# Seven products for eight in the down projection of an encoder step's feed-forward part, with new block closings and buffers

## The chip, the cores and the metric

The kernel runs on one core of one Trainium2 chip. Its time is the device time of one execution in microseconds. The engines that matter here are TensorE (PE, the matrix products; PEld in the profile is its loading of stationary operands), VectorE (DVE), ScalarE (ACT), GpSimd (POOL) and the queue of SyncE (SP), which issues nearly all transfers. Work on an engine runs in the order in which it was placed in that engine's queue.

## The reference, cut to what matters

One layer of a streaming encoder is computed for 2048 prompt tokens and 32 sample tokens, 2080 in all, with a model width of 1024 and a feed-forward width of 2816. Each of its three sub-layers has a norm before and a norm after, and is added to the residual:

```python
xp = xp + rmsnorm(mix_output(oa, ob, r, g_gla_out[l], w_o[l]), g_post_mix[l])
...
xp = xp + rmsnorm(mem_attention(rmsnorm(xp, g_pre_mem[l]), mk, mv, w_mq[l], w_mo[l]), g_post_mem[l])
...
def swiglu(h, w_gate, w_up, w_down):
    return (jax.nn.silu(h @ w_gate) * (h @ w_up)) @ w_down
xp = xp + rmsnorm(swiglu(rmsnorm(xp, g_pre_ffn[l]), w_ffn_gate[l], w_ffn_up[l], w_ffn_down[l]), g_post_ffn[l])
```

The change lies in the last of these, the feed-forward part, and in the few lines before it that end the memory attention. Everything is in 32-bit floats.

## The kernel before, in words

Every large product is made of three: each operand is split into a rounded part (type fp32r) and the remainder, and `mm3` (L130 to L137) issues high by high, high by low and low by high. `split` (L77 to L82) makes the two parts: ACT casts (L78), and DVE or POOL subtracts (L82). Where no engine is named, `lo_set` and `flip` let POOL and DVE take turns.

The feed-forward part starts at L1018. Tokens are in three blocks (`CF`), and each block is two halves of 348 or 346 tokens, called `ci` 0 and 1. Activations are feature-major: features on the 128 partitions, tokens along the row. The feed-forward width is 22 tiles of 128 features, taken as 11 groups `g` of two tiles.

For a group, `gate_up` makes the gate product and the up product. Each of them is one `unit` (L1117): a 2 by 2 block product by the seven-product scheme (Strassen's in Winograd's form), over two row halves and two column halves of the weights, and two feature halves and two token halves of the activations. The seven combinations of the activations are made once per block (`ffn_ops`, tiles `mf`, from the loaded `hr`). The seven combinations of the weights are made for each unit (`unit_w`: the raw tiles `wg_r` and `wu_r` are changed in place by four sums on DVE, lines L1039 and L1042, and split seven times into `wg_s` and `wu_s`, 512 columns each). Each of the seven products is 12 matmuls into PSUM banks X, Y and Z; the first three values are copied out by ACT (L1122 to L1126, tile `pg_c` or `pu_c`), the next ones are summed by DVE. After the up unit, DVE multiplies the four quarters (L1150, `sg`), and each is split into `u`, with POOL making the remainder.

`down` (L1177) adds a group to the block's accumulator `acc` in the plain way: for each token half and each of the 8 output tiles, 6 matmuls (two feature tiles by three products) into one bank, and a DVE sum into `acc` straight from PSUM (L1042; a copy, L1185, for the first group). That is 96 matmuls for a group, 288 for a group with its two units, so 264 with the seven-product units: 84 for gate, 84 for up, 96 for down. The loop emits the down product of group g-1 after the units of group g.

At the end of blocks 0 and 1, `finish` closes the block for each token half: squares on ACT, their sum on DVE (`ssq`), a matmul with ones, the root, the scaling (DVE, L1222), the residual (`x2r`, added by POOL), a transposition to token-major rows by PE (`yt`, L1230, with the copies out of PSUM at L1231), and the store. In the last block the second half closes the same way and the first one by `finish_rows`, which transposes before it scales.

The order within each queue is set when the program is built: a planner runs the emitted instructions by priority through a timeline of its own and places each when its operands would be ready. `high_priority` raises a block of code; weights have it. So down products are used as filler between the matmuls of the units.

SBUF is laid out by pools in the order in which they are opened. The feed-forward pools lie over those of the memory attention, so a tile's place decides which earlier work it has to wait for.

Of the kernel before, what the change touches and what calls it, by code (L numbers as in the profile page):

```python
# [45 lines left out]
def encoder_step(ctx, tc, ins, outs):  # L46
# [806 lines left out]
    with ExitStack() as ph:  # L853
# [149 lines left out]
        out = []  # L1003
        for b in range(len(CB)):
            mo, heads = mem_attn(b)
            fill = [partial(mem_q, b + 1, mv, m) for m in range(KT)] if b + 1 < len(CB) else out
# [4 lines left out]
            out = mem_out(b, mo)  # L1011
            if b != len(CB) - 2:
                for it in out:
                    it()
# [5 lines left out]
    UB, WRB, WSB, SGB = 3, 4, 8, 5  # L1020
    with ExitStack() as ph:
        def pool(name, bufs):
            return ph.enter_context(tc.tile_pool(name=name, bufs=bufs, **RW))
# [10 lines left out]
        pd = ph.enter_context(tc.tile_pool(name="cpd", bufs=6, space=PSUM, **RW))  # L1034
# [9 lines left out]
        def stage(name):  # L1044
            return gp.tile([P, HK, 348], F32, tag="stage", name=name)

        def ffn_raw(b):

            s, n = CF[b]
            raw = {}  # L1050
            for kh, c in ((0, 0), (0, 1), (1, 1), (1, 0)):
# [6 lines left out]
        def ffn_ops(b, raw):  # L1058

            n = CF[b][1]  # L1060
            b11, b12, b22, b21 = raw[0, 0], raw[0, 1], raw[1, 1], raw[1, 0]
            ops = []

            def put(src, eng):
                m_ = mps[len(ops)].tile([P, 2, HK, 348], F32R, tag="mov", name=f"mf{b}_{len(ops)}")
                split(m_[:, 0, :, :n], m_[:, 1, :, :n], src, eng)
                ops.append((m_[:, 0, :, :n], m_[:, 1, :, :n]))

# [10 lines left out]
            put(b21, DVE)  # L1079
            return ops  # L1080

        def unit_w(src, g, name):

            with tc.high_priority(offset=PRI):
                raw = []
                for kh in range(2):
                    r = wp.tile([P, HK, 2, P], F32, tag="wraw", name=f"{name}_r{kh}", bufs=WRB)
                    SP.dma_start(r, src[kh * 512 : kh * 512 + 512, g * 256 : g * 256 + 256].rearrange("(k p) m -> p k m", p=P).rearrange("p k (a m) -> p k a m", a=2))
                    raw.append(r)
                a11, a21, a12, a22 = raw[0][:, :, 0], raw[0][:, :, 1], raw[1][:, :, 0], raw[1][:, :, 1]  # L1090
                ops = []

                def put(v, eng=None):
                    w = wp.tile([P, 2, HK, P], F32R, tag="wsp", name=f"{name}_s{len(ops)}", bufs=WSB)
                    split(w[:, 0], w[:, 1], v, eng)
# [15 lines left out]
        def prod(ps, w, m, first, last):  # L1111
            mm3(ps, [((w[0][:, k], w[1][:, k]), (m[0][:, k], m[1][:, k])) for k in range(HK)], first, last, not first)

        def small(pool, tag, name, bufs):
            return pool.tile([P, 348], F32, tag=tag, name=name, bufs=bufs)

        def unit(w, m, n, name, dst):  # L1117

            X, Y, Z = (pd.tile([P, 512], F32, tag="dense", name=f"{name}_{c}")[:, :n] for c in "XYZ")
            cp = [small(sp, "cp", f"{name}_c{i}", 4)[:, :n] for i in range(3)]  # L1120
            prod(X, w[0], m[0], True, True)
            ACT.copy(cp[0], X)  # L1122
            prod(Y, w[1], m[1], True, True)
            ACT.copy(cp[1], Y)
            prod(X, w[2], m[2], False, True)
            ACT.copy(cp[2], X)  # L1126
            prod(Y, w[3], m[3], False, True)
            add(DVE, dst[0, 1], cp[2], Y)
            prod(X, w[4], m[4], False, True)
            add(DVE, dst[1, 1], cp[1], X)  # L1130
            prod(Z, w[5], m[5], True, True)
            add(DVE, dst[0, 0], cp[0], Z)
            prod(X, w[6], m[6], False, True)
            return X

        QS = ((0, 1), (1, 1), (0, 0), (1, 0))
        ops = ffn_ops(0, ffn_raw(0))
        for b, (s, n) in enumerate(CF):
            ssqs, silu = {}, []
            acc = [xp.tile([P, KT, 348], F32, tag="acc", name=f"acc{b}_{ci}") for ci in range(2)]  # L1140
            def gate_up(g, own=False):
                sg = {q: small(sp, "sg", f"sg{b}_{g}_{q[0]}{q[1]}", SGB)[:, :n] for q in QS}
                up = {q: small(up_, "up", f"up{b}_{g}_{q[0]}{q[1]}", 3)[:, :n] for q in QS[:3]}
                X = unit(unit_w(ins["w_ffn_gate"][0], g, f"wg{b}_{g}"), ops, n, f"pg{b}_{g}", sg)
                for q in QS:
                    silu.append(ACT.activation(sg[q], sg[q] if q != (1, 0) else X, AF.Silu))
                up[1, 0] = unit(unit_w(ins["w_ffn_up"][0], g, f"wu{b}_{g}"), ops, n, f"pu{b}_{g}", up)
                u = [(gp if own else uu).tile([P, 2, 2, 348], F32R, tag="stage" if own else "u", name=f"u{b}_{g}_{j}") for j in range(2)]
                for q in QS:
                    DVE.tensor_tensor(out=sg[q], in0=sg[q], in1=up[q], op=ALU.mult)  # L1150
                    ut = u[q[0]][:, :, q[1], :n]
                    split(ut[:, 0], ut[:, 1], sg[q], POOL)
                return u

            def down_w(f):

                row = []
                with tc.high_priority(offset=PRI):
                    raw_d = wp.tile([P, KT, P], F32, tag="wraw", name=f"wd{b}_{f}_r", bufs=WRB)
                    SP.dma_start(raw_d, ins["w_ffn_down"][0][f * P : (f + 1) * P, :].rearrange("p (k m) -> p k m", k=KT))  # L1160
                    for q in range(2):
                        w = wp.tile([P, 2, HK, P], F32R, tag="wsp", name=f"wd{b}_{f}_{q}", bufs=WSB)
# [4 lines left out]
            def square(ci, m):  # L1167

                if m == 0:
                    ssqs[ci] = small(np_, "nacc", f"ssq{b}_{ci}", 2)[:, :n]  # L1170
                    ACT.activation(ssqs[ci], acc[ci][:, m, :n], AF.Square)
                else:
                    sq = small(np_, "nsq", f"sq{b}_{ci}_{m}", 1)[:, :n]
                    ACT.activation(sq, acc[ci][:, m, :n], AF.Square)
                    add(DVE, ssqs[ci], ssqs[ci], sq)

            def down(gs, us, cis=(1, 0), dn=None):  # L1177
                dn = dn or [down_w(2 * g + j) for g in gs for j in range(2)]
                us = [ut for u in us for ut in u]
                for ci in cis:  # L1180
                    for m in range(KT):
                        ps = pd.tile([P, 512], F32, tag="dense", name=f"pdn{b}_{gs[0]}_{m}_{ci}")
# [169 lines left out]
```

## Time and profile before

| What | Value |
|---|---|
| median of 3 runs | 3489.44 us (3487.72 to 3491.62) |
| the profiled execution | 3487.48 us, its span 3485.7 us |
| mean granted TensorE clock | 0.974 |
| PE busy over the span | 3305.2 us (95%) |
| DVE, ACT, POOL busy | 2351.4, 1671.8, 1320.4 us (67%, 48%, 38%) |
| first and last feed-forward product | 1994.0 us, 3463 us after the span's start |

In the profile a line of a group names source line, engine, operation, the tile written and the tiles read, shapes and count, busy time and mean duration, and then the idle time before it and what ended that. A helper's line (L78, L82, L137, L1039, L1042) is shared by all that use it, so tiles tell more than lines. In a table of stretches each engine has its busy time and, in brackets, the number of its instructions; PEclk is the granted clock.

### The profile page before, as it was taken

What the parts mean: (1) busy time and instruction counts of PE and PEld (TensorE: products, weight loads), DVE (VectorE), ACT (ScalarE), POOL (GpSimd) and SP (SyncE); (2) the same over time, 40 slices, a digit from 0 to 9 for tenths busy, and PEclk for the clock granted to TensorE, in tenths of its full rate; (3) what the DMA queues carried; (4) which work ended last, traced back from release to release, by engine and by line L of the source; (5) the groups of instructions that cost most, each with busy time, mean ns of one, the idle gap of its engine ahead of it and who ended that gap; (6) DMA issues with size and microseconds to landing.
All of it is one profiled execution on the core that took longest, in us unless ns stands there. A gap on an engine that the chain in (4) does not pass through costs nothing. (4 is left out here: it accounts for less than half of the span.)

```text
span 3485.7 us, 60212 instructions
## 1 busy us (share of the span) xinstructions
PE 3305.2 (95%) x22211; PEld 3113.8 (89%) x22211; DVE 2351.4 (67%) x4395; ACT 1671.8 (48%) x3733; POOL 1320.4 (38%) x1086
## 2 busy tenths in 40 slices
PE   7999999999998989899999789999899999999998
PEld 6888988989987778789999689999899999899998
DVE  4578687664567887486666685666976657866665
ACT  4455455453455555465555443334543334533334
POOL 3233232132144434344533453333453334533332
PEclk9999999999999989999999899999999999999999
DMA  8865664555446555665645542222242223222222
GB/s 248 261 214 169 188 184 139 165 172 158 125 145 203 173 169 172 200 210 161 187 144 167 172 136 79 73 73 74 94 138 73 79 77 92 93 91 73 73 73 90
DMA packets 550044, 488.56 MB, mean 140 GB/s; under 512 B 48488, under 2 KB 496801, under 8 KB 549749
## 3 DMA queue, kind: packets, MB, share of 16 engines
q1 hardware_dynamic: 549749, 484.71, 45.2%
q8 instruction: 174, 2.85, 0.3%
q14 instruction: 121, 0.99, 0.1%
HBM read 369.68 MB, written 114.91 MB: 139 GB/s over the span
## 5 line engine op out<-in xcount | busy, mean ns | idle before, releaser
L137 PE MATMUL pdn<-u,wd 128*128 128x346 f32 (+1 forms) x3168 | 526.0, 323 | 13.1 <-DVE up L1042 9.8
L137 PEld LDWEIGHTS pdn<-u,wd 128*128 128x128 f32 x3168 | 509.7, 190 | 15.7 <-DVE up L1042 10.4
L78 ACT CAST wg_s<-wg_r 128x512 fp32r<-128x512 f32 x231 | 139.5, 620 | 410.7 <-PE pdn L137 198.6
L137 PE MATMUL pg_X<-mf,wg_s 128*128 128x346 f32 (+1 forms) x1584 | 282.4, 327 | 8.7 <-DVE mf L82 3.1
L1042 DVE TENSOR_TENSOR acc<-acc,pdn 128x346 f32<-128x346 f32 (+1 forms) x464 | 231.1, 510 | 87.2 <-PE pdn L137 87.1
L137 PE MATMUL pu_X<-mf,wu_s 128*128 128x346 f32 (+1 forms) x1584 | 282.2, 323 | 0.0
L137 PEld LDWEIGHTS pg_X<-mf,wg_s 128*128 128x128 f32 x1584 | 259.4, 192 | 12.7 <-ACT mf L78 4.1
L137 PEld LDWEIGHTS pu_X<-mf,wu_s 128*128 128x128 f32 x1584 | 257.9, 190 | 0.4
L82 POOL TENSOR_TENSOR wu_s<-wu_r,wu_s 128x512 fp32r<-128x512 f32 x132 | 176.3, 1336 | 210.2 <-ACT wu_s L78 202.6
L82 POOL TENSOR_TENSOR wg_s<-wg_r,wg_s 128x512 fp32r<-128x512 f32 x99 | 136.0, 1375 | 302.6 <-ACT wg_s L78 291.9
L137 PE MATMUL wops<-om,wo_s 128*128 128x512 f32 (+1 forms) x960 | 209.0, 366 | 16.0 <-ACT om L78 9.3
L137 PE MATMUL wvr_ps<-wvr_s,mv 128*128 128x256 f32 (+3 forms) x1632 | 216.5, 286 | 1.2 <-DVE wvr_s L82 1.2
L82 POOL TENSOR_TENSOR u<-sg,u 128x346 fp32r<-128x346 f32 (+1 forms) x132 | 135.0, 1033 | 198.6 <-ACT u L78 198.6
L137 PE MATMUL mops<-mo,wmo_s 128*128 128x416 f32 x960 | 199.9, 358 | 5.9 <-DVE wmo_s L82 4.4
L137 PEld LDWEIGHTS wvr_ps<-wvr_s,mv 128*128 128x128 f32 (+1 forms) x1632 | 200.6, 183 | 4.7 <-DVE wvr_s L82 1.4
L137 PEld LDWEIGHTS wops<-om,wo_s 128*128 128x128 f32 x960 | 158.4, 196 | 41.6 <-ACT om L78 10.5
L137 PEld LDWEIGHTS mops<-mo,wmo_s 128*128 128x128 f32 x960 | 179.1, 191 | 11.1 <-DVE wmo_s L82 5.4
L78 ACT CAST wu_s<-wu_r 128x512 fp32r<-128x512 f32 x231 | 136.3, 618 | 89.3 <-DVE wu_r L1042 34.0
L137 PE MATMUL mqps<-m,wmq_s 128*128 128x416 f32 x768 | 165.9, 365 | 6.1 <-DVE wmq_s L82 6.1
L442 PE MATMUL po<-prt,v 128*128 128x128 f32 x1120 | 168.4, 281 | 0.8 <-ACT prt L493 0.7
L411 ACT ACTIVATE u_sb<-u_sb,u_mn 128x640 f32<-128x640 f32 (+4 forms) x128 | 97.6, 763 | 120.4 <-DVE u_mn L408 120.0
L442 PEld LDWEIGHTS po<-prt,v 128*128 128x128 f32 x1120 | 150.2, 195 | 5.4 <-ACT prt L493 1.1
(410 smaller groups left out, 7911.0 us busy)
## 6 DMA issues: line engine op xcount, KB each, us to landing
wg_r<-in_w_ffn_gate_dram SPq DMA_DIRECT2D x66, 512.0 KB, 3.7
wu_r<-in_w_ffn_up_dram SPq DMA_DIRECT2D x66, 512.0 KB, 4.0
wd_r<-in_w_ffn_down_dram SPq DMA_DIRECT2D x66, 512.0 KB, 3.5
wmq_r<-in_w_mq_dram SPq DMA_DIRECT2D x80, 256.0 KB, 2.8
wmo_r<-in_w_mo_dram SPq DMA_DIRECT2D x80, 256.0 KB, 2.9
wo_r<-in_w_o_dram SPq DMA_DIRECT2D x64, 256.0 KB, 3.1
ks<-kad SPq DMA_DIRECT2D x28, 512.0 KB, 5.6
wvr_r<-in_w_in_dram SPq DMA_DIRECT2D x48, 256.0 KB, 3.7
```

The lines of the kernel that those rows point to most:

```text
L78: ACT.copy(hi, src)
L82: lo_eng.tensor_tensor(out=lo, in0=src, in1=hi.bitcast(F32), op=ALU.subtract)
L137: PE.matmul(ps, lhsT=a, rhs=b, start=first and i == 0, stop=last and i == len(seq) - 1, skip_group_check=skip)
L411: ACT.activation(sbv, sbv, AF.Exp, bias=mn[:nq, 0:1], scale=-1.0, accum_out=mn[:nq, 1:2])
L442: PE.matmul(po[:, e * P : e * P + n], lhsT=v[:kk, j, :], rhs=prt[:kk, j, :n], start=j == 0, stop=j == len(rows) - 1)
L1042: eng.tensor_tensor(out=out, in0=a, in1=b, op=ALU.add)
```

## The change

Groups 0 to 7 are taken in pairs, and the down product of a pair is made by the seven-product scheme too. Over the two groups it is a 2 by 2 block product: two tiles j of each group against two halves of the output features, and two token halves. `u_seven` makes seven combinations of a group's four quarters (four DVE sums in place, seven splits with the remainder on POOL) where `u_plain` makes four splits. `down_pair` runs for two output quarters `h`; for each it loads and combines weights (`seven_w`, the former `unit_w`), and issues seven products for two output tiles r, 6 matmuls each. The first three values are copied out by ACT and added into `acc` by POOL (for the first pair ACT copies straight into `acc`); the other four are added by DVE from PSUM. Groups 8, 9 and 10 stay plain. A pair's down product is emitted after the gate unit of the next group.

The closing of blocks 0 and 1 becomes five pieces (`closing`), two squares or four scalings each, emitted between the units of the next block's first three groups; odd sums and residuals are on POOL. There are no transpositions in it: y leaves feature-major (`y_t`), and is rearranged on the host; only the last half (`y_l`) is stored in rows. PSUM banks are handed out by hand in rotation (`banks`), results leave PSUM at a raised priority (`out`), the pools have another order and other sizes, the first block's operands are made at a raised priority, and the end of the memory attention loses its raised one.

```diff
@@ mem_fin @@
-            with tc.high_priority(offset=2 * PRI if last else 0):
+            if True:
...
-    UB, WRB, WSB, SGB = 3, 4, 8, 5
+    NG = NF // 2
+    WRB, WSB, SGB, CPB, GPB = 4, 7, 5, 6, 7
...
-        mps = {i: pool(f"cm{i}", 1) for i in (5, 6)}
-        gp = pool("cg", 4)
-        wp = pool("cw", 4)
-        uu = pool("cu", UB)
-        sp = pool("cs", 4)
-        mps.update({i: pool(f"cm{i}", 1) for i in (4, 0, 1, 2, 3)})
-        up_ = pool("cp", 3)
-        np_ = pool("cn", 1)
-        xp = pool("cx", 2)
+        mps = {i: pool(f"cm{i}") for i in (4, 6)}
+        sp = pool("cs")
+        mps.update({i: pool(f"cm{i}") for i in (0, 1)})
+        wr = pool("cwr")
+        gp = pool("cg")
+        mps.update({i: pool(f"cm{i}") for i in (2, 3, 5)})
+        np_ = pool("cn")
+        ws = pool("cws")
+        up_ = pool("cp")
+        xp = pool("cx")
...
+        def out(f, *a):
+            with tc.high_priority(offset=2 * PRI):
+                f(*a)
...
+        def seven(make, n, name, copies, sums):
+            R = range(len(copies))
+            use = [f"{c}{r}" for c in "XYZ" for r in R]
+            ps = banks(use, [f"{c}{r}" for c in "YZX" for r in R], name)
+            ps = {c: t[:, :n] for c, t in ps.items()}
+            for i, c in enumerate("XYXYXZX"):
+                first = i in (0, 1, 5)
+                for r in R:
+                    mm3(ps[f"{c}{r}"], make(i, r), first, True, not first)
+                for r in R:
+                    if i < 3:
+                        copies[r](i, ps[f"{c}{r}"])
+                    else:
+                        sums[r](i, ps[f"{c}{r}"])
...
-        ops = ffn_ops(0, ffn_raw(0))
+        raw = ffn_raw(0, ((0, 0), (0, 1), (1, 1), (1, 0)))
+        with tc.high_priority(offset=PRI):
+            ops = ffn_ops(0, raw)
...
+            def u_seven(g, sg, home):
+                res = []
+                def put(src, _):
+                    ...
+                    split(t[:, 0, i, :n], t[:, 1, i, :n], src, POOL)
+                    res.append((t[:, 0, i, :n], t[:, 1, i, :n]))
+                seven_mov(sg, put)
+                return res
...
+            def down_pair(g, us):
+                for h in range(2):
+                    srcs = ...
+                    w = seven_w(srcs, f"wd{b}_{g}_{h}")
+                    def make(i, r):
+                        return [((w[i][0][:, k, r * P : r * P + P], w[i][1][:, k, r * P : r * P + P]), us[k][i]) for k in range(2)]
...
+                    def copies(r):
+                        def f(i, ps):
+                            to = dst({2: (0, 1), 1: (1, 1), 0: (0, 0)}[i], r)
+                            if g == 0:
+                                out(ACT.copy, to, ps)
+                            else:
+                                c = small(sp, "cp", f"pd{b}_{g}_{h}_{r}_c{i}", CPB, n)
+                                out(ACT.copy, c, ps)
+                                out(add, POOL, to, to, c)
+                        return f
+                    def sums(r):
+                        def f(i, ps):
+                            to = dst(SUM[i], r)
+                            if g == 0 and i == 6:
+                                out(DVE.tensor_copy, to, ps)
+                            else:
+                                out(add, DVE, to, to, ps)
+                        return f
+                    seven(make, n, f"pdn{b}_{g}_{h}", [copies(0), copies(1)], [sums(0), sums(1)])
...
+            def closing(b=b, s=s, n=n, acc=acc, ssqs=ssqs, square=square):
+                def sq(ci, m):
+                    for mm in (m, m + 1):
+                        square(ci, mm, POOL if mm % 2 else DVE)
...
+                def scale(ci, k0):
+                    a, c0 = acc[ci], s + ci * n
+                    for k in (k0, k0 + 1):
...
+                        DVE.scalar_tensor_tensor(out=a[:, k, :n], in0=a[:, k, :n], scalar=gains["g_post_ffn"][:, k : k + 1], in1=ssqs[ci], op0=ALU.mult, op1=ALU.mult)
+                        add(POOL, a[:, k, :n], a[:, k, :n], xr)
+                    SP.dma_start(outs["y_t"][k0 * P : k0 * P + 2 * P, c0 : c0 + n].rearrange("(k p) n -> p k n", p=P), a[:, k0 : k0 + 2, :n])
+                one = [partial(sq, ci, m) for ci in (1, 0) for m in range(0, KT, 2)]
+                two = [partial(scale, ci, k) for ci in (1, 0) for k in range(0, KT, 2)]
+                return [one[:4], one[4:] + [stats], two[:3], two[3:6], two[6:]]
...
+            todo, plain, pair = [], {}, []
+            for g in range(NG):
+                sg = gate(g)
+                rest()
+                for f in todo:
+                    f()
+                todo = []
+                up(g, sg)
+                if g < NG - 3:
+                    if g % 2 == 0:
+                        home, pair = [], []
+                    pair.append(u_seven(g, sg, home))
+                    if g % 2:
+                        todo = [partial(down_pair, g - 1, pair)]
+                else:
+                    plain[g] = u_plain(g, sg)
+                    if g == NG - 3:
+                        todo = [partial(down, [g], [plain[g]])]
+                rest()
```

More of the change, by code (lines that the diff above doesn't have):

```diff
@@ L1109, in unit_w @@
             return ops
[L1111 to L1134, printed above, removed]
@@ L1138, in encoder_step @@
+        raw = ffn_raw(0, ((0, 0), (0, 1), (1, 1), (1, 0)))
+        with tc.high_priority(offset=PRI):
+            ops = ffn_ops(0, raw)
+        late = []
         for b, (s, n) in enumerate(CF):
+            last = b == len(CF) - 1
             ssqs, silu = {}, []
[L1140 to L1144, printed above, removed]
-                for q in QS:
[L1146 to L1152, printed above, removed]
-                return u
```

224 lines of the change are left out of this document (138 added, 86 removed).

## The prediction

> **What bounds the kernel now.** I read the page's busy shares first, then the table of stretches over the feed-forward part, then the waits at its start, then the order of DVE and POOL inside one steady stretch.
>
> ```profile
> PE 3305.2 (95%) x22211; PEld 3113.8 (89%) x22211; DVE 2351.4 (67%) x4395; ACT 1671.8 (48%) x3733; POOL 1320.4 (38%) x1086
> ...
> 1988.00:2080.00 92.00, 68.50 (x377) 63.41 (x378) 78.54 (x84) 46.43 (x77) 48.14 (x30) 0.87 0.52 163
> 2100.00:2440.00 340.00, 340.00 (x2140) 340.00 (x2139) 207.93 (x349) 133.16 (x264) 127.67 (x106) 1.00 0.25 75
> 2440.00:2490.00 50.00, 43.45 (x259) 42.27 (x258) 49.74 (x62) 23.13 (x37) 24.04 (x14) 0.93 0.30 91
> 2490.00:2560.00 70.00, 63.21 (x380) 59.64 (x379) 60.09 (x76) 40.10 (x75) 43.34 (x34) 0.95 0.33 109
> ...
> 2990.00:3060.00 70.00, 63.24 (x382) 59.86 (x381) 61.91 (x80) 34.99 (x67) 44.90 (x36) 0.95 0.37 122
> 3080.00:3420.00 340.00, 340.00 (x2144) 340.00 (x2143) 207.27 (x348) 133.32 (x264) 128.79 (x107) 1.00 0.25 78
> ```
>
> Columns are the stretch, its length, then PE, PEld, DVE, ACT, POOL, the clock, DMA. Inside a block PE is never idle: 340.00 of 340 us, 2140 products, so 0.1589 us for each, and every product that goes is worth that. At the block ends it is otherwise: from 2490 to 2560 only 328 of the 380 are products (the stretch's matmuls of line L137), 52.1 us worth, so 17.9 of 70 us are lost; 17.2 in the second closing; 8.8 and 9.0 in the 50 us ahead of them (259 and 258 products); 32.7 of the 92 us at the start (373 products). DVE is busy 86% there and POOL 62%, against 61% and 38% in the steady stretch.
>
> ```profile
> PE pg_Y L137 <- ACT mf L78: 11.2, 1, 11.2
> ACT mf L78 <- DVE hr L1039: 11.4, 3, 7.5
> ```
>
> At the start PE waits for the first block's operands, which DVE combines.
>
> ```profile
> 2283.87 0.94 POOL L82 TENSOR_TENSOR u<-sg,u 128x348 fp32r<-128x348 f32 x1
> 2296.58 1.47 POOL L82 TENSOR_TENSOR wg_s<-wg_r,wg_s 128x512 fp32r<-128x512 f32 x1 [4.30 <-ACT wg_s L78]
> ...
> 2283.95 1.41 DVE L1039 TENSOR_TENSOR wg_r<-wg_r,wg_r 128x512 f32<-128x512 f32 x1 [0.83 <-POOL wg_s L82]
> 2296.22 0.68 DVE L82 TENSOR_TENSOR wg_s<-wg_r,wg_s 128x512 fp32r<-128x512 f32 x1
> 2297.70 0.52 DVE L1042 TENSOR_TENSOR acc<-acc,pdn 128x348 f32<-128x348 f32 x1 [0.37 <-PE pdn L137]
> ```
>
> This decides the case. The DVE sum over two SBUF tiles, 0.68 us alone, took 1.41 because it began under POOL's `u`, and ended 0.55 us after it (2285.36 against 2284.81). POOL's `wg_s` took 1.47 because DVE held until 2296.90, and ended 1.15 after that. The sum that reads PSUM took 0.52 under POOL's instruction: it does not wait. So POOL's instructions and DVE's with two SBUF inputs take turns, one at a time. Adding up, from the records, the time in which one of the two held its turn: 0.65 of the steady stretch from 2100 to 2400, but 0.87 to 0.90 of the 60 us windows in the closings, where PE lost 17.
>
> **The change, part by part.** The base is the profiled execution, 3487.48 us (span 3485.7 and 1.8 around it), 2.0 below the median of the runs.
>
> Products. A pair's plain down product is 2 x 96 matmuls; in the new form 2 quarters x 7 products x 2 tiles x 6, so 168. Four pairs in three blocks: 12 x 24 = 288 fewer, 288 x 0.1589 = -45.8 us. A pair with its four units needs 504 x 0.1589 = 80.1 us of PE, 83.9 before.
>
> What hides the added work. For a pair, the turns on the common resource: POOL 21 weight remainders (half of 28 for the units and 14 for the down weights), 14 of `u` and 12 additions into `acc`; DVE 21 remainders, 24 weight sums, 8 sums of `u` and 6 multiplications. In strict alternation each holds, by the rows above, POOL 1.15 (512 columns), DVE 0.55; for 346 columns the records give 0.79 and 0.38. So 21 x 1.15 + 26 x 0.79 + 45 x 0.55 + 14 x 0.38 = 74.8 us. Back to back the pitches are 1.25, 0.90, 0.61 and 0.43: 83.1 us. The same counts for two groups of before (18 and 8, 34 and 6) give 48.0 and 53.0 us, and the trace has 0.65 x 83.9 = 54.5. So the need rises from 65% of PE's time to between 93 and 104%. Where both engines always have work they alternate, so I take 74.8, and 0.90 as the share of time that can be held, the best that the closings show over 60 us: 74.8 / 0.90 = 83.1 us, 3.0 over PE's 80.1, for nine pairs (the first pair of a block has no additions): +27. Ends: 0 if the planner packs it without gaps, and 83.1 / 0.90 = 92.3, +110, if it never alternates.
>
> DVE's own queue loses 32 sums of 0.43 us pitch and gains 16 for a pair, so that alone would be lighter; ACT gains 14 - 8 casts for the down weights (0.62), 14 - 8 for `u` (0.48) and 12 copies (0.45), 12 us in 80, at 39% busy: no cost, as long as its copies don't queue behind a cast that waits for DVE. The third copy of each tile has to be added by POOL before DVE's next sum into the same part of `acc`, 1.9 us of products later; with POOL behind by one instruction that sum waits, and all of DVE's queue behind it. That is part of why I take no value under 0.90. The down weights come in 8 loads a pair of 256 KB rather than 4 of 512; at 3.5 us to landing, two sets ahead, no cost.
>
> Closings of blocks 0 and 1. They leave PE's queue: 48 transpositions each at some 0.09 us (x8 took 0.7 to 0.8 us in a row), 4.3 us. But their turns stay, and gain: POOL 24 of 346 columns, DVE 22, 24 x 0.79 + 22 x 0.41 = 28 us, between the next block's first gate unit and its first pair, since that pair's copies need `acc`, which has two buffers. That stretch has 5 units and 14 products of down, 93 us of PE, and needs 7 x 8.2 (seven weight sets) + 2.3 + 14.1 (`u`) + 28 = 101.8 of turns, 113 at 0.90. Before, its PE share was 97 us and 17.9 were lost: 115. Of the 3.8 us of products already counted nothing is left there: 113 - 115 + 3.8 = +2 each, +4. Ends: -25 (all hidden) to +25. The stores of y wait in SP's queue for POOL's addition, with weight loads behind them; two sets of raw weights ahead (26 us) cover that, and if they don't, a unit starts late by the few us of that wait. The 17.8 us ahead of the closings stay: their cause, the operands of the next block, is not touched.
>
> Start. `hr` is moved to where attention's last tiles are free early, and so are the first two `mf`; their chain starts before the last `mops` matmul, so the 11.2 us wait goes. What is late next: the norm of the last attention block, moved behind it, takes 22 us of turns (8 additions and 14 square sums, 16 scalings of 416 columns) that must be done before the first pair. 95 us of turns against 93 of PE, 106 at 0.90: 13 lost, and 5 for the third to fifth operand. 32.7 - 18 = 15 gained; ends 0 and 26.
>
> Tail. The second half of the last block needs no `yt`: 32 transpositions and the idle 2.2 us before 3466.18 lie ahead of the last sums. I take -5, ends 0 and -9.
>
> Sum: 3487.5 - 45.8 + 27 + 4 - 15 - 5 = 3452.7, say 3453.
>
> **The rivals.**
> PE stays the bound. DVE and POOL are each under 75% by their own work, and a gap-free alternation needs 74.8 of 80.1 us. Then nine pairs cost nothing, the closings lose as much as before, the start gains 20: 3487.5 - 45.8 - 20 - 5 = 3417, 3395 with hidden closings. Against it: no 60 us window of the trace held above 0.73 without loss of product time.
>
> Slower: the turns decide in the pairs. If a pair takes 89 us (74.8 held 0.84 of the time, or 80 held 0.90), nine cost +80: 3453 - 27 + 80 = 3506, and with 10 more from closings 3516. It decides from a pair of 87.0 us on, where nine times 6.9 eat the 45.8 + 15 + 5 - 4. For it: the closings, with the same mix, held 0.87 and starved PE; the 12 additions of a pair read PSUM on DVE before, without a turn, and take one on POOL now. Against it: the closings are a chain of few instructions, the pairs have 14 us of weights ahead.
> On this the Trainium skill, Perfetto Trace Analysis, "Optimizing Scalar/DVE Operations", says that POOL and DVE share an SBUF read port, so that moving work between those two might not help. By that rule the additions moved to POOL save DVE nothing, as this rival has it; the rows at 2283.95 and 2296.58 agree with the sharing, and no row of before shows what the move is worth.
>
> The change does not reach what it aims at outside the pairs: the closing holds `acc` until the first pair and PE stands there for 10 us in two blocks, and the start gains nothing, because `hr` still waits for transfers behind weights: 3453 + 20 + 15 = 3488, no change.
>
> **How the numbers follow.** Forecast (some turns exposed, 3430 to 3480) 0.43; PE bound, 3395 to 3430, 0.25; slower, 3495 to 3530, 0.22; no change 0.10. 0.2% is 7 us, about what a measurement of this kernel tells from no change. Faster takes 0.25, 0.41 of the forecast, 0.01 and 0.02 of the others: 0.69; same 0.02 + 0.02 + 0.04: 0.08; slower 0.23. The range leaves out the lower half of the second and the top of the third: 3400 to 3515.
>
> **What would show it.** Stretches inside a block: if PE is busy all the time and a pair takes 80 us, the second case; if PE waits for `wu_s`, `wg_s`, `wd` or DVE's sums, with DVE over 85% and POOL over 65%, the forecast, and its size is the pair's length over 80.1. The products must count 288 fewer. After 2490 the loss should lie before the first pair, not at transpositions. At the start the wait for `mf` should be short. I am wrong if ACT's copies or POOL's additions, not the turns, hold PE, or if the planner's order puts weights late where turns are free.

## The result and the profile after

The changed kernel takes 3540.99 us (median of four runs, 3538.09 to 3544.68), the kernel before 3489.14 beside it (3487.72 to 3491.62). The ratio is 1.0148, with a 95% interval of 1.0131 to 1.0166: slower by 1.5%, and outside the predicted range. The profiled execution took 3542.59 us, its span 3540.8, so 55.1 us more than the span of before.

The engines' line of the page, changed kernel:

```profile
PE 3281.5 (93%) x21795; PEld 3066.3 (87%) x21795; DVE 2552.6 (72%) x4399; ACT 1777.9 (50%) x4005; POOL 1656.4 (47%) x1318
```

PE has fewer instructions and a smaller share; DVE is busier (67% before), and above all POOL (38% and 1086 instructions before). The table of stretches, changed kernel (stretch, length, then PE, PEld, DVE, ACT, POOL, clock, DMA):

```profile
1990.00:2034.00 44.00, 3.67 (x6) 1.30 (x6) 34.85 (x29) 16.70 (x21) 22.77 (x11) 0.56 0.35 114
2034.00:2126.00 92.00, 85.52 (x510) 83.36 (x511) 72.35 (x93) 45.34 (x94) 47.88 (x36) 0.95 0.27 86
2180.00:2430.00 250.00, 235.50 (x1417) 228.98 (x1416) 197.66 (x249) 117.56 (x251) 175.41 (x136) 0.98 0.24 75
2540.00:2630.00 90.00, 75.32 (x424) 71.03 (x423) 76.86 (x91) 45.83 (x90) 63.50 (x51) 0.92 0.40 122
```

There are two new places. PE stands still for some 40 us after the memory attention (first row), where before it began at 1994.0 us. And inside a block (third row), where PE had no idle time at all, it now loses 25 of 250 us: 1417 matmuls at 0.1588 us are 225. The closing (last row) still loses time, as it did before.

To put numbers on places I count **lost time**: the time since the attention's last `mops` matmul, less 0.1588 us for each feed-forward product started so far. Read at the same product counts, it says where each kernel loses time:

| Stretch, by count of products | before | changed |
|---|---|---|
| attention's last `mops` matmul ends at | 1987.9 us | 1989.8 |
| start, to product 500 | 33.1 lost | 55.1 |
| inside blocks (800 to 2400, 3600 to 5200, 6400 to 8000) | 0.4, 0.0, 0.0 | 25.6, 25.2, 25.6 |
| the two closings (2400 to 3600, 5200 to 6400) | 27.5, 27.2 | 29.8, 28.1 |
| 8000 to the last product | 3.8 | 3.5 |
| last product to the end of the span | 22.6 | 20.4 |
| products | 8712 | 8424 |

The differences: 288 products fewer, -45.7; blocks +76; start +22; closings +3; attention's end +2; the rest -2.5. They add up to the 55 us between the spans.

**The start.** The waits of PE from 1985 to 2040 us, changed kernel:

```profile
PE n_ps L100 <- POOL n_acc L98: 38.4, 2, 35.9
PE pg_X L137 <- DVE wg_s L82: 3.8, 1, 3.8
PE pg_X L137 <- ACT wg_s L78: 1.8, 1, 1.8
```

The 11.2 us wait for `mf` is not among them, since no product asks for `mf` before 2032.6 us; the first cast of `mf` starts at 1991.0 us, only 1.6 earlier than before. PE's next instruction is now the ones-matmul of the norm behind the last attention block, and the first gate product stands behind it. ACT shows where the gate weights were placed (timeline of ACT, changed kernel):

```profile
2030.90 0.61 ACT L86 ACTIVATE n_r<-n_ps,eps_t 128x416 f32<-128x416 f32 x1 [2.98 <-PE n_ps L100]
2031.54 0.55 ACT L87 ACTIVATE n_r<-n_r 128x416 f32<-128x416 f32 x1
2031.99 0.60 ACT L78 CAST wg_s<-wg_r 128x512 fp32r<-128x512 f32 x1
```

The first cast of the first gate weights comes directly behind that norm's last root. Its raw weights had been asked for at 1958 us. In the new layout the pool of the split weights ends at byte 200928 of a partition, and the pool of that norm's buffers begins at 200832: one of the seven slots that the first gate unit fills shares 96 bytes with the norm, and the planner placed all seven casts in ACT's queue behind it.

**Inside a block.** POOL, DVE and PE around one of the new idle times (timelines of the three engines, changed kernel):

```profile
2194.71 1.26 POOL L82 TENSOR_TENSOR wd_s<-wd_r,wd_s 128x512 fp32r<-128x512 f32 x1 [1.33 <-ACT wd_s L78]
2195.93 0.92 POOL L82 TENSOR_TENSOR u<-sg,u 128x348 fp32r<-128x348 f32 x1
...
2196.01 1.39 DVE L1041 TENSOR_TENSOR wd_r<-wd_r,wd_r 128x512 f32<-128x512 f32 x1 [1.66 <-POOL wd_s L82]
2197.32 0.50 DVE L1044 TENSOR_TENSOR sg<-pg_c,pg_X 128x348 f32<-128x348 f32 x1
...
2192.78 2.07 PE L137 MATMUL pdn_Y<-u,wd_s 128*128 128x348 f32 x12
2197.88 2.18 PE L137 MATMUL pg_X<-mf,wg_s 128*128 128x348 f32 x12 [3.02 <-DVE sg L1044]
```

Read it from the end. PE waits 3.02 us for a DVE sum that only empties a bank (`sg<-pg_c,pg_X`). That sum takes 0.50 us, but it stands in DVE's queue behind a weight sum (`wd_r`) that first waits 1.66 us for POOL's remainder, then takes 1.39 us, because POOL's `u` began 0.08 us before it and the two take turns. The waits of PE from 2172 to 2452 us, the inside of block 0:

```profile
PE pg_X L137 <- DVE sg L1044: 6.9, 3, 3.0
PE pu_X L137 <- DVE acc L1044: 3.3, 3, 1.6
PE pdn_Z L137 <- DVE wd_s L82: 1.7, 2, 0.9
PE pdn_Z L137 <- ACT wd_s L78: 1.4, 2, 0.7
...
```

These and two of 0.4 us are 14.1 of the 25.6 us lost; the rest are gaps too short to be listed, and a granted clock of 0.98 instead of 1.00.

### The profile page after: what moved, and what is told of

Its sections match the earlier page's. It is cut to its first block, busy times and chain, and to the rows that moved or that the text cites. A ratio compares the mean times of both kernels' runs of the same rounds, so it can differ in the third digit from the quotient of the medians.

```text
span 3540.8 us, 60198 instructions
## 1 busy us (share of the span) xinstructions
PE 3281.5 (93%) x21795; PEld 3066.3 (87%) x21795; DVE 2552.6 (72%) x4399; ACT 1777.9 (50%) x4005; POOL 1656.4 (47%) x1318
## 4 chain that ended last, share of the span: by engine, by line
PE 50%; DVE 20%; POOL 10%; issue 9%; ACT 6%; DMA 4%; SPq 1%; POOLq 0%; ACTq 0%; DVEq 0%
PE mops L137 5%; PE wops L137 5%; PE pdn_X L137 4%; PE wvr_ps L137 4%; POOL u L82 3%; PE wva_ps L137 3%; PE mqps L137 2%; PE po L442 2%; PE wqa_ps L137 2%; PE wka_ps L137 2%; POOL acc L1044 2%; PE pu_X L137 2%; DVE sg L1041 2%; PE s L437 2%; DVE wu_r L1041 1%
## 5 line engine op out<-in xcount | busy, mean ns | idle before, releaser
L82 POOL TENSOR_TENSOR u<-sg,u 128x346 fp32r<-128x346 f32 (+1 forms) x204 | 245.6, 1223 | 81.3 <-ACT u L78 81.3
L82 POOL TENSOR_TENSOR wu_s<-wu_r,wu_s 128x512 fp32r<-128x512 f32 x132 | 192.0, 1460 | 141.5 <-ACT wu_s L78 127.3
L137 PE MATMUL pdn_X<-u,wd_s 128*128 128x346 f32 (+1 forms) x1152 | 203.6, 322 | 6.5 <-DVE acc L1044 4.2
L137 PEld LDWEIGHTS pdn_X<-u,wd_s 128*128 128x128 f32 x1152 | 185.7, 188 | 10.6 <-DVE acc L1044 6.9
L82 DVE TENSOR_TENSOR wg_s<-wg_r,wg_s 128x512 fp32r<-128x512 f32 x132 | 162.8, 1244 | 22.2 <-ACT wg_s L78 21.8
L78 ACT CAST wd_s<-wd_r 128x512 fp32r<-128x512 f32 x168 | 97.6, 620 | 131.2 <-DVE wd_r L1041 78.5
L137 PE MATMUL pu_Y<-mf,wu_s 128*128 128x346 f32 (+1 forms) x792 | 146.3, 331 | 14.6 <-ACT wu_s L78 14.0
```

The source lines that it names most:

```text
L78: ACT.copy(hi, src)
L82: lo_eng.tensor_tensor(out=lo, in0=src, in1=hi.bitcast(F32), op=ALU.subtract)
L137: PE.matmul(ps, lhsT=a, rhs=b, start=first and i == 0, stop=last and i == len(seq) - 1, skip_group_check=skip)
```

## The experiments

Two groups: the start (three runs), and the loss inside the blocks (thirteen). Among the latter stands one version more, with what was learned up to there, which the last five runs start from. The edits are against the changed kernel unless another is named. Where no interval is given, a kernel ran once. Beside these runs the kernel before alone took 3485.8 to 3501.4 us, so the argument goes by the lost time inside each trace and not by times a few us apart. "Held" is the share of time in which POOL, or DVE with a two-input sum from SBUF, had its turn, worked out from the records as in the prediction: 0.65 in the blocks of before, 0.868 in those of the changed kernel. "Per pair" is per 504 products of the blocks.

### The start: 96 bytes

```diff
-        np_ = pool("cn")
         ws = pool("cws")
+        np_ = pool("cn")
```

> The changed kernel with two pools in the other order, so that the split weights (cws) end below the buffers of the attention's last norm, which they overlap by 96 bytes per partition in the changed kernel. Theory (placement): the planner holds all weights of the first gate unit behind that norm because of these 96 bytes; with the swap the first products come some 35 to 39 us earlier, and the time is 3502 to 3508 us. Rival (the norm's lost priority is what delays the start): 3541, no change.

Measured: 3533.69 us (3532.91 to 3535.83), 1.0122 of before (1.0100 to 1.0144). The first feed-forward product starts at 1999.5 us instead of 2032.6 and 41.9 us are lost to product 500 instead of 55.1. The first product came 33 us earlier, as expected, but the shared bytes cost only 13 us of lost time there, and 7 in all, since attention ended 4 us later in this build; 3502 to 3508 was missed. The other stalls stayed: what PE then waited for was `wu_s` and `mf`.

### The start: the priority of the last norm

```diff
-            if True:
+            with tc.high_priority(offset=2 * PRI if last else 0):
```

> The changed kernel with the raised priority of the attention's last closing put back, pools as in the changed kernel. Theory (placement): first feed-forward product still at about 2032 us, time 3541 within 5. Rival (priority): first product near 1994, time near 3505.

Measured: 3544.75 us, first product at 2035.6, 55.2 us lost to product 500. The norm's lost priority is not the cause.

### The start: the whole layout

```diff
         mps = {i: pool(f"cm{i}") for i in (4, 6)}
         sp = pool("cs")
-        mps.update({i: pool(f"cm{i}") for i in (0, 1)})
         wr = pool("cwr")
         gp = pool("cg")
-        mps.update({i: pool(f"cm{i}") for i in (2, 3, 5)})
-        np_ = pool("cn")
+        mps.update({i: pool(f"cm{i}") for i in (0, 1, 2, 3, 5)})
         ws = pool("cws")
+        np_ = pool("cn")
```

> The changed kernel with its pools in another order: the stages for the activations and the raw weights right above the small tiles, then the seven operand pools, then the split weights, the norm's buffers last. By the built order the first gate unit's weights and all loads of the first block then wait for nothing that runs to the end of the attention. Theory (placement decides the start): lost time from the end of attention to the 500th feed-forward product falls from 55 us to 15 to 25, time about 3505. Rival (the turns of norm, operands and weights are the limit there, whatever the places): as with the two pools swapped, some 42 us lost, time about 3534.

Measured: 3530.31 us. The first product starts at 1993.6, before the attention's last matmul has ended, and 36.5 us are lost to product 500. The first cast of `mf` starts at 1971.9 us here, 19 earlier than in the changed kernel. The placement therefore costs 18.6 us there. But the loss falls neither to the 15 to 25 us that were expected nor below that of before. The waits of PE from 1994 to 2090 us in this kernel:

```profile
PE pg_X L137 <- DVE mf L82: 5.5, 1, 5.5
PE pu_X L137 <- DVE up L1043: 5.4, 1, 5.4
PE pg_Y L137 <- POOL wg_s L82: 2.6, 1, 2.6
PE pg_Y L137 <- DVE y L979: 2.2, 1, 2.2
...
```

An early first product is followed by waits for the same DVE and POOL work; held is 0.92 there.

### The blocks: the additions into `acc` off POOL

```diff
-                                c = small(sp, "cp", f"pd{b}_{g}_{h}_{r}_c{i}", CPB, n)
-                                out(ACT.copy, c, ps)
-                                out(add, POOL, to, to, c)
+                                out(add, DVE, to, to, ps)
```

> The changed kernel, with the first three values of each product tile added into acc by DVE straight from PSUM, as the other four are, in place of ACT's copy and POOL's addition. Theory (turns): a pair loses 12 turns of 0.79 to 0.90 us, its need falls from 75 to 83 us to 65 to 72, and at a held share of 0.90 that is 72 to 80 us, under PE's 80.1; nine pairs lose under 2 us each instead of some 8, time 3470 to 3490. Rival (DVE's own queue or the planner's order is the limit): DVE gets 12 more instructions a pair (5 us), so the time stays at 3541 or rises.

Measured: 3497.78 us. Lost inside the blocks: 12.8, 11.8, 11.9, together 36.5 instead of 76.4; held 0.81. Taking 108 additions from POOL gave 40 us, 0.37 us for each, although DVE got 108 sums more (82% busy in the blocks instead of 78%). That is 8 us above what was expected if this were all of it: half of the blocks' loss remained.

### The blocks: the remainders of `u` off POOL

```diff
-                    split(t[:, 0, i, :n], t[:, 1, i, :n], src, POOL)
+                    split(t[:, 0, i, :n], t[:, 1, i, :n], src, DVE)
```

> The changed kernel with only the remainders of u moved from POOL to DVE; ACT's copies and POOL's additions are kept. Theory (turns): the time held in a pair falls from 76.5 to about 70.6 us, the loss from 8.1 to 3 or 4 us a pair, time about 3498. Rival (the chain copy, POOL addition, DVE sum into the same part of acc): the chain is untouched and DVE has more to do, so 3541 or more.

Measured with the additions left on POOL: 3507.91 us, 18.4, 14.3 and 13.4 lost inside the blocks, held 0.84 to 0.86. The move of 168 subtractions from POOL to the busier DVE gave 30 us in these stretches, where 105 of them lie; 4.8 us per pair are still lost, where 3 or 4 were expected.

Both edits together:

> The kernel without POOL additions (e3_no_pool_adds), with the remainders of a pair's u made by DVE instead of POOL. Theory A (what is left lost in the pairs, 4 us each, is still the turns): a pair's turns fall by 14 x 0.4 = 5.7 us, the loss by 3 to 4 us a pair, time about 3468. Theory B (what is left is DVE's own queue, 81% busy there): DVE gets 14 x 0.43 = 6 us a pair more, the loss grows to 8 us or more a pair, time 3530 or more.

Measured: 3475.54 us, 3.5, 3.5 and 3.6 lost inside the blocks, held 0.79, DVE 84% busy, POOL 39%. The stretch of the changed kernel's third row, in this one:

```profile
2180.00:2430.00 250.00, 249.82 (x1556) 247.13 (x1554) 212.39 (x346) 111.27 (x225) 98.06 (x68) 1.00 0.26 78
```

DVE is busier than in the changed kernel (212 us to 198), POOL much less (98 to 175), and PE is full. So it wasn't DVE's own load. The two movements to POOL account for 66 of the 76 us.

### The blocks: plain down products with all the rest of the change

```diff
-                if g < NG - 3:
+                if g < 0:
...
-                    if g == NG - 3:
+                    if g <= NG - 3:
```

Beside this, the first group's sum is a copy, as it was before.

> The changed kernel with all eleven groups taken by the plain down product (288 products more), its closings, pools and priorities kept. Theory (turns): inside a block PE loses nothing, held share back at about 0.65; 45.8 us more of products, some 75 us less lost: about 3512 us. Rival (the closings or the new layout cause the loss inside the blocks): 3541 + 46 = 3587 us.

Measured: 3523.93 us. Inside the blocks 1.1, 0.6 and 0.6 us are lost, held 0.64, as before. At the start 49.7, and the closings cost 36 each rather than 27.5, so the small steps of the closing are no shorter by themselves. The blocks' loss belongs to the pairs alone.

### A full POOL in the kernel before

Two things can be meant by "POOL is in the way": it takes turns, or its results come late. In the kernel before, POOL got work that nobody needs, in the tiles `sg` after their last use:

```diff
+                for q in QS + QS + QS:
+                    add(POOL, sg[q], sg[q], sg[q])
```

> The kernel before, with 12 additions more on POOL in each group (each adds a finished quarter sg to itself; the value is not used afterwards). Nothing but POOL's own queue and the turns depends on them. Theory (turns): the held share goes from 0.65 to about 0.89, PE begins to lose 1 to 3 us in each group, time 3525 to 3590. Rival (in the changed kernel it is the chain copy, POOL addition, DVE sum that costs): no change, 3489.

Measured: 3512.24 us. Held rose to 0.805, POOL to 69%, and nothing was lost inside the blocks; the 18 us more that were lost lie at the start (39.4) and in the closings (32 and 35).

The same with fills, `POOL.memset(sg[q], 0.0)` in place of the addition:

> The kernel before, with 12 fills of the same quarters on POOL in each group, which read nothing from SBUF. Theory (turns, for the reading of two tiles): DVE's sums are not held up, no change, 3489. Rival (POOL's queue being longer is what costs): as slow as with the 12 additions, as far as the fills take as long.

Measured: 3499.02 us, a fill 0.39 us; no loss inside the blocks. Both runs were too mild, so both were repeated with more, 18 additions or 42 fills in a group.

> The kernel before with 18 unused POOL additions in each group instead of 12. At 12 the blocks lost nothing at a held share of 0.80. Theory (turns): 18 take the need past 0.87, PE loses inside the blocks too, 2 to 6 us in a group, time 3570 to 3700. Rival (a held share near 0.9 alone does no harm, it is the seven-product form): no loss inside the blocks, 3520.

> The kernel before with 42 fills on POOL in each group, 0.39 us each by the run with 12, so POOL has as much more to do as with 18 additions, but reads nothing for it. Theory (turns): no loss inside the blocks, 3495 to 3510. Rival (POOL's busy queue delays the weights' remainders): as slow as with 18 additions.

Measured: 3530.11 us with the additions, 3510.65 with the fills. Stretches of the kernel with 18 additions, then DVE's `wu_s` remainders in it (count, duration in ns as minimum, median, maximum):

```profile
2200.00:2400.00 200.00, 200.00 (x1259) 200.00 (x1258) 147.21 (x209) 76.36 (x153) 157.98 (x146) 1.00 0.25 77
```

```profile
L82 DVE TENSOR_TENSOR wu_s<-wu_r,wu_s x14: 676/1210/1435, 2203.8 to 2372.8; 128x512 fp32r<-128x512 f32 x14
```

The same two views of the kernel with 42 fills:

```profile
2200.00:2400.00 200.00, 200.00 (x1260) 200.00 (x1260) 126.86 (x209) 78.37 (x154) 143.01 (x254) 1.00 0.26 77
```

```profile
L82 DVE TENSOR_TENSOR wu_s<-wu_r,wu_s x14: 691/694/1686, 2200.3 to 2370.3; 128x512 fp32r<-128x512 f32 x14
```

The same remainders in the kernel before:

```profile
L82 DVE TENSOR_TENSOR wu_s<-wu_r,wu_s x15: 691/692/1364, 2221.9 to 2395.9; 128x512 fp32r<-128x512 f32 x15
```

Two readings. Additions delay DVE: its remainder takes 1.21 us instead of 0.69, and fills, with POOL nearly as busy, leave it at 0.69. On this the Trainium skill, SBUF — State Buffer, "Who interferes with whom", says that a DVE instruction with two inputs from SBUF contends with a GpSimd instruction that reads SBUF and not with one that only writes it; the trace agrees (1210 ns beside additions, 694 beside fills). And yet PE has 200.00 of 200 us: held is 0.90 here, over stretches of 50 products as much as 1.00, and inside the blocks nothing is lost. The changed kernel loses 8.0 us per pair at 0.87. So the share itself, on which the prediction had rested its 0.90, is not the limit. What these two runs lose more than before lies elsewhere: 14 us at the start and 26 in the closings with the additions, 13 and 9 with the fills. At the start the fills cost as much as the additions, so turns don't explain that part.

### Layout and both movements together

The edits of the runs on the whole layout, the additions and the remainders of `u`, in one kernel:

> The changed kernel with the pools of v4_layout, no POOL additions (e3_no_pool_adds) and the remainders of u on DVE (e8_u_on_dve). If the parts add up: e8's 3475.5 less the 18 us that the layout saved at the start, 3450 to 3465 us, 0.8 to 1% under the kernel before. If the start is bound by the turns of the norm and the operands whatever the layout, 3475.

Measured: 3458.14 us (3457.01 to 3459.30, four runs), 0.9892 of before (0.9875 to 0.9908): faster than both kernels. Its stretches at the start and inside block 0:

```profile
1994.00:2090.00 96.00, 76.24 (x401) 71.38 (x400) 86.67 (x103) 52.12 (x92) 48.76 (x28) 0.89 0.32 101
2180.00:2430.00 250.00, 249.68 (x1547) 245.78 (x1546) 206.15 (x331) 108.53 (x219) 103.06 (x72) 1.00 0.29 86
```

33.2 us are lost to product 500, the same as before, 13 inside the blocks, 28.0 and 27.0 in the closings. Of the 45.7 us of products, 28 reach the span: 12.6 go to the blocks, and attention ends 6.6 us later in this build.

### Turns in the form of seven products, with no reader

That left open whether in the new form turns alone cost time, or the wait for POOL's results (`u` and `acc` are both read). The kernel for it is the one just described, with the new layout and without the two movements to POOL (3458.14 us; 1.4 us lost per pair). It gets idle additions into a scratch tile:

```diff
+        dum = xp.tile([P, 348], F32, tag="dum", name="dum", bufs=1)
+        POOL.memset(dum, 0.0)
...
                 seven_mov(sg, put)
+                for _ in range(6):
+                    add(POOL, dum, dum, dum)
```

> Both movements undone and the pools placed anew, as in the run of 3458.1 us (held share 0.79, 1.4 us lost per pair), and then POOL adds a scratch tile to itself 12 times per pair (6 per group of the pairs, 348 columns); nobody reads the tile. Theory of turns in the form of seven products: the 12 additions hold 12 x 0.79 = 9.5 us of the pair's 80, the share comes to about 0.88 to 0.91, and 5 to 10 us are lost per pair, as in the changed kernel at 0.87: 3458 + 9 x 3.6 to 9 x 8.6 = 3490 to 3535. Rival, the chain: what cost time was that DVE's next sum and the products waited for POOL's result itself (acc, u). Here nobody waits for it, so 1 to 2 us per pair and 3455 to 3468.

With 18 fills of the tile, `POOL.memset(dum, 0.0)`, instead:

> As the run with 12 idle additions, but with 36 fills of the scratch tile per pair (18 per group, 0.39 us each), which read nothing. POOL is then as busy as with the additions, or busier (36 x 0.39 = 14 us per pair). Turns: a fill takes none, 1 to 2 us per pair, 3455 to 3468. If POOL's busy time itself (its remainders coming late) is what costs: as with the additions, 3490 or more.

With 12 additions instead of 6:

> As the run with 12 idle additions per pair, but 24. Turns: 24 x 0.79 = 19 us more of holding in 80, a need of 0.79 + 0.24 = 1.03, which cannot be met: the pair grows to at least 63.5 + 19 = 82.5 held at 0.87 to 0.90, so 92 to 95 us, 12 to 15 lost per pair, 3458 + 9 x 10.6 to 13.6 = 3553 to 3580. Chain: 3455 to 3475.

Measured: 3520.62, 3468.58 and 3567.29 us. The doses were not the planned ones. As nothing tied the instructions to their group, the planner ran them all ahead: the 144 additions lie between 2057 and 2339 us, the 432 fills between 2054 and 2372, the 288 additions between 2054 and 2655. So the per-pair figures of the expectations can't be read from them, but the price of one instruction can. Stretches with 144 additions, then with 432 fills:

```profile
2200.00:2340.00 140.00, 123.29 (x683) 114.37 (x683) 127.44 (x161) 50.78 (x102) 115.53 (x102) 0.94 0.20 61
```

```profile
2200.00:2340.00 140.00, 137.47 (x849) 134.80 (x848) 120.54 (x188) 64.64 (x132) 122.06 (x233) 1.00 0.26 77
```

POOL is busier with the fills, 122 of 140 us, and PE makes 849 matmuls there; beside the additions it makes 683. Over the whole feed-forward part the lost time rose from 104.9 us to 163.2, 111.8 and 211.9: 0.40 us for an addition, 0.02 for a fill, 0.37 for an addition again. Nobody reads these results, and POOL is busier with the fills, so the turns of the additions are enough to stop PE.

To set the dose, each addition then read a prepared operand of its own group, `add(POOL, dum[:, :n], res[i % 7][0], res[i % 7][0])`, 6 in a group and then 9:

> As the run with 12 idle additions per pair, but each of the 6 of a group adds a prepared operand of that group's u into the scratch tile, so that they can't be run ahead into block 0 as they were there (some 56 per pair from 2060 to 2340, with 21 us lost per pair; fills 115 per pair, 3 us lost). Turns in the form of seven products: 12 per pair bring the held share from 0.79 to 0.87 to 0.91, where the changed kernel stood, and 3 to 9 us are lost per pair: 3480 to 3530. If a share near 0.9 costs no more in this form than it did in the plain form, where 18 additions per group held 0.90 without a loss: 1 to 2 us per pair and 3455 to 3470, and the loss of the changed kernel came from POOL's results being waited for.

> As the run before it with 18 such additions per pair. Turns: 6 more x 0.79 = 4.7 us of need, so the pair grows by up to that over 0.9: 6 to 14 us lost per pair, 3505 to 3575. Otherwise 3455 to 3475.

Measured: 3522.66 and 3550.34 us. Lost inside the blocks: 18.5, 19.5, 18.6 with 12 additions per pair (6.0 per pair), 23.7, 22.2, 23.6 with 18 (7.3 per pair), against 4.9, 4.0, 4.1 without. Held is only 0.81 and 0.83. Over the whole feed-forward part that is 0.48 and 0.42 us for each addition. The time is lost where the additions stand close together and nowhere else: of the first run's stretches of 100 products from 800 to 2400, those with four to six additions lost 2.2 to 4.5 us, those with two or fewer 0.8 or less. One such place in the run with 12 per pair, its stretch and then POOL, DVE and PE:

```profile
2224.00:2240.00 16.00, 13.55 (x82) 12.74 (x82) 15.11 (x22) 6.40 (x16) 9.23 (x9) 1.00 0.22 67
```

```profile
2231.93 4.22 POOL L1043 TENSOR_TENSOR dum<-u 128x348 f32<-128x348 f32 x4 [2.08 <-ACT u L78]
...
2231.82 2.53 DVE L82 TENSOR_TENSOR u<-sg,u 128x348 fp32r<-128x348 f32 x3
2234.27 0.50 DVE L1043 TENSOR_TENSOR sg<-pg_c,pg_Y 128x348 f32<-128x348 f32 x1
2234.70 0.82 DVE L82 TENSOR_TENSOR wu_s<-wu_r,wu_s 128x512 fp32r<-128x512 f32 x1
...
2235.58 1.71 PE L137 MATMUL pu_Y<-mf,wu_s 128*128 128x348 f32 x9 [1.66 <-DVE wu_s L82]
2238.08 2.19 PE L137 MATMUL pg_X<-mf,wg_s 128*128 128x348 f32 x12 [0.79 <-DVE sg L1043]
```

Four idle additions run on POOL from 2231.93 to 2236.15; in that time DVE's three remainders of `u` take 2.53 us, DVE is busy 15.11 of 16 us, its next remainder of the weights is 1.66 us late for PE, and PE stops. POOL itself is busy only 9.23 of 16 us.

## Why the prediction was wrong, step by step

**Products, -45.8: right.** 288 fewer, 45.7 us at 0.1588.

**What hides the added work, +27: mis-sized, and this decided the sign.** The measured term is +76. The 1600 products read in each block are 3.17 pairs, so a pair takes 88.1 us, not 83.1, and loses 8.0, not 3.0; put on the nine pairs with additions, all of which lie in these stretches, the loss is 8.5 each. The step was right that turns are what the added work costs (additions without a reader bring the loss back, fills don't), and in their amount: 0.868 of 88.1 us is 76.5, against 74.8. It failed where it turned the 74.8 us of turns into a time, by "0.90 as the share of time that can be held, the best that the closings show". The share held doesn't set the time: the plain form held 0.90 for whole blocks at no loss, and the seven-product form lost 6.0 us per pair at 0.81. What the runs give in its place is a price for each instruction moved in the new form: 0.37 us for each of the 108 additions put on POOL (40 us, or 0.33 and 35 us with the `u` remainders already on DVE), 0.29 for each of the 105 remainders of `u` in the same stretches that POOL has rather than DVE (30 us, or 0.25 and 26 us without the additions), 0.37 to 0.48 for an idle addition. The nearest number of before was the 0.55 us by which DVE's sum at 2283.95 outlasted POOL's `u`: for 108 additions 59 us, against the 40 measured, and far from the 27 for everything.

The rival "slower" named this outcome, its threshold of 87.0 us per pair and its price of 89: 88.1 to 88.6 was measured, and the total was higher than its 3506 to 3516 because the start lost too.

Also in this step: ACT's 12 us more were taken at no cost. That isn't measured by itself. Undoing the additions took their ACT copies away as well, so the 0.37 us holds for both; the idle additions, which have no copy, cost as much.

**Closings, +4: right in sum, by two errors that nearly offset each other.** Measured are +2.3 and +0.9. The 17.8 us ahead of the closings were to stay; from product 2400 to the block's end, and from 5200 in the second block, 6.1 and 5.3 us are lost instead of 9.3 and 9.0. Behind the block's end it is 23.7 and 22.7 us instead of 18.2 each, 5 more, where the sum had 2. With plain groups the same closings cost 36 each, so how they fit depends on what runs beside them.

**Start, -15: wrong in sign, +22.** The loads of `hr` did move, from 1986.1 us on to 1975.2 on, but "their chain starts before the last `mops` matmul" did not happen: the first cast of `mf` started 1.2 us after that matmul's end, at 1991.0 us against 1992.6 before. The wait is missing only because the first product came 39 us later. In the run on the whole layout that cast started at 1971.9. What was late wasn't only the norm's turns, as the step had it, but the first gate weights, which had been ready early before and now share 96 bytes with that norm's buffers. The prediction looked at where the moved buffers went and not at what came to lie in the places next to them. With the layout mended 18.6 us come back by product 500, but even the best run loses 33.2 us there, as much as before. So the gain of 15 was wrong as well: even with its chain begun 20 us earlier, PE waits for the later `mf` and for other work of DVE and POOL, at 0.92 held.

**Tail, -5: half.** The last product to the end became 2.2 us shorter, and 0.3 us less is lost ahead of it.

**Not in the sum:** attention's last matmul ended 1.9 us later, and among the builds between 1985.5 and 1997.6 us, with no edit in attention but, in one of them, the priority of its last norm. So a start or end of a few us in a single build proves nothing; the lost time is counted from that matmul for this reason.

With the two wrong terms replaced, 3487.5 - 45.7 + 76 + 3 + 22 + 2 - 2.5 is 3542, the profiled execution's time.

On moving work between the two engines the prediction named the Trainium skill, Perfetto Trace Analysis, "Optimizing Scalar/DVE Operations", by which it might not help: the trace agrees, with 40 us lost by the move of the additions. In the other direction, the remainders of `u` from POOL to DVE, a move gave 30.

**What stays open.** Why the plain form takes bursts of turns without loss and the new form doesn't. Two things differ: in the plain form DVE is less loaded (147 of 200 us with 18 additions, against 173 in the seven-product run with 12 per pair), and its down products are short runs of 6 matmuls, each into a bank of its own, so that PE may have other work ready. No run changed one of these alone. DVE's load is at any rate not the whole of it: the changed kernel lost 8.0 us per pair with DVE at 78%, the best one 1.4 at 84%.

## What to carry to other kernels

Before work is moved to POOL beside a DVE that sums two SBUF tiles, price each moved instruction as a delay of DVE in the place where it will stand, and look at what PE has ready there; a mean share of held or busy time says little, since 0.90 was free in one form and 0.81 cost 6 us in 80 in another. If a result can be read from PSUM by DVE, leave it there: a sum from PSUM waited for no turn here (beside 18 additions per group, DVE's 112 sums into `acc` from 2100 to 2400 us took 0.50 to 0.52 us each). When buffers are laid out anew, compare byte ranges across the phase boundary for every pool, those that were not moved on purpose too.

## What the runs showed of the hardware that was not expected

- POOL's fill of 128x348 takes 0.39 us, and 42 of them per group, with POOL at 72%, left DVE's remainders at 0.69 us. Additions of that size, 18 per group, took 0.92 us in the median of 594 and delayed the remainders to 1.21.
- POOL and DVE held their common turn for 0.90 of the time through whole blocks, and 1.00 of it over 50 products, with PE full at a clock of 1.00.
